# A two-block transformer on one core: wider loads of the experts' down weights, and a different last stretch

## The chip, the cores and the metric

The kernel runs on one core of one Trainium2 chip. The metric is the device time of one launch in microseconds (us), the median of several runs.

## The reference

The program is one layer of each of two transformer blocks on 256 tokens of width 1024, in float32. The change touches only the last part, a mixture of 16 experts (`ec_moe`) and the final normalization:

```python
x = x + ec_moe(rmsnorm_2(x, norm_ffn_g), router_w, expert_w_gu, expert_w_down)
return rmsnorm_2(x, final_norm_g)

def ec_moe(h, router_w, w_gu, w_down):        # h: 256 x 1024, 16 experts, cap = 32 tokens for each
    aff = softmax(h @ router_w)
    gates, idx = top_k(aff.T, cap)            # each expert picks its 32 tokens
    xs = h[idx]                               # 16 x 32 x 1024
    for each expert e:
        ga, up = split(xs[e] @ w_gu[e])       # w_gu[e]: 1024 x 4096, 16 MB
        y[e] = (silu(ga) * up) @ w_down[e]    # w_down[e]: 2048 x 1024, 8 MB
    return scatter-add of gates * y to the picked tokens
```

All 16 experts work, so 384 MB of expert weights are read once.

## The kernel before

`Body.run` goes through block 1, block 2's mixers and cross attention, and then `moe` (from L1209). In `moe` the 32 tokens of an expert are the stationary operand and the weights stream through TensorE, so that each weight is read once by a matmul of 512 columns. Four such matmuls sit side by side in the array (`tile_position=(0, 32 * j)`).

For each expert the code (L1271 to L1367) does the following.
- Every fourth expert gathers the tokens of four experts with one-hot matmuls (`gather`, L1284) into `xs`.
- Gate and up weights (`w_gu`): from the third expert on, four loads of 4 MB (L1303), each giving every partition 32 KB in one piece. Each load feeds 32 matmul instructions (L1314; a float32 matmul is two instructions in the trace).
- SiLU on ScalarE (L1334), the product on VectorE (L1335), four transposes of 128 x 128 (L1338) and a copy give `aT`, the activations with features on partitions. Feature `512 j + 4 p + c` of the expert lies on partition p, block c.
- Down weights (`w_down`): four loads of 2 MB (L1365), each giving every partition 16 KB. `down` (L1342) feeds each to 16 matmul instructions (L1347), which sum into two PSUM banks `y`.
- `scatter` (L1355): the two banks are copied to SBUF, one by ScalarE (L1357), one by VectorE (L1359), and a one-hot matmul with the gates (L1361) adds them into four PSUM banks `acc` that stay open over the experts.

`eload` (L1228) issues each load from SyncE, which here does nothing but issue DMAs, in program order. A load waits until the last reader of its buffer is done. Buffers come from `slots`: four of 32 KB per partition (`e_`) and four of 16 KB (`hl`, the pool `big` that block 1 and 2 used). One expert uses each once.

The order of the other instructions on each engine is made by a scheduler at build time. `queued` and `issue_after` put an instruction behind a named one, and `strict` keeps program order on PE, VectorE and ScalarE.

The last expert (e = 15) is different. After expert 14, `acc` is added to `x` on VectorE (L1374). The gain row of the last normalization is loaded and spread over partitions (L1377 to L1381). Then the down weights come as two loads of 2 MB (j = 0, 1), and j = 2 and 3 in column pieces: `cuts` are 512, 256, 128 and 128 columns (L1386, L1401). For each cut the result goes through `scatter`, is added to `x` (L1410), squared and summed (L1411). After the last cut VectorE works out the reciprocal root of both token blocks together by a bit trick and three Newton steps (`rstd`, L1415), ScalarE scales the left half and VectorE the right half (L1417, L1418), and two DMAs write the output (L1420).

Of the kernel before, what the change touches and what calls it, by code (L numbers as in the profile page):

```python
# [9 lines left out]
F32 = mybir.dt.float32  # L10
# [22 lines left out]
class Body:  # L33
# [223 lines left out]
    def rstd_q(self, ss):  # L257

        nc = self.nc
        q = self.small.tile([128, 8], F32, name="rstq", tag="rsq", bufs=4)  # L260
        v, d, h, y, t = (q[:, i:i + 1] for i in range(5))
        nc.vector.tensor_scalar(v, ss[:, 0:1], ss[:, 1:2], 1.0 / D, OP.add, OP.mult)
        nc.scalar.activation(d, v, AF.Sqrt, bias=self.eps)
        nc.vector.tensor_scalar(h, v, -0.5, -0.5 * EPS, OP.mult, OP.add)
        nc.vector.reciprocal(y, d)
        nc.vector.tensor_scalar(t, y, y, h, OP.mult, OP.mult)
        nc.vector.tensor_scalar(y, t, 1.5, y, OP.add, OP.mult)
        return y
# [29 lines left out]
    def run(self):  # L298
# [10 lines left out]
        self.big = self.open("big", 1)  # L309
# [896 lines left out]
    def moe(self):  # L1206
# [3 lines left out]
        with ExitStack() as es:  # L1210
            ep, x = self.ep, self.x
            ew = self.open("ew", 1, es)
# [58 lines left out]
            for e in range(NE):  # L1271
                q = e % 4
                if q == 0:
# [60 lines left out]
                nc.scalar.activation(s, G, AF.Silu, scale=rs)  # L1334
                nc.vector.scalar_tensor_tensor(s, U, rs, s, OP.mult, OP.mult)  # L1335
                p = self.ps()
                for c in range(4):
                    nc.tensor.transpose(p[:, c * 128:(c + 1) * 128], s[:, c:512:4], self.ident)  # L1338
                aT = ew.tile([128, 4, 128], F32, name="aT", tag="aT")
                nc.scalar.activation(aT.rearrange("p c s -> p (c s)"), p, AF.Copy)  # L1340
# [8 lines left out]

                def rows(j):  # L1350
                    return wdn[e, 512 * j:512 * j + 512].rearrange("(p i) n -> p i n", i=4)


                def scatter(c0, n, out, first, last):
                    ys = ew.tile([128, n], F32, name="ys", tag="ys")  # L1355
                    if c0 == 0:
# [3 lines left out]
                    for t in range(2):  # L1360
                        nc.tensor.matmul(out[t], ogT[:, t * 128:(t + 1) * 128], ys, start=first, stop=last)  # L1361

                if e < NE - 1:
                    for j in range(4):
                        raw = eload(rows(j).rearrange("p i n -> p (i n)"))  # L1365
                        for n in range(2):
                            down(j, raw, 512 * n, 512)  # L1367
                    for n in range(2):
                        scatter(512 * n, 512, acc[n::2], e == 0, e == NE - 2)

            for t in range(2):
                for n in range(2):
                    c = slice(512 * n, 512 * n + 512)
# [94 lines left out]
```

## Time and profile before

| | us |
|---|---|
| median of 3 runs (lowest to highest) | 1518.48 (1516.9 to 1519.0) |
| profiled execution, its own device time | 1518.31 |
| span of the profiled execution, first to last instruction | 1516.6 |
| PE busy | 1162.6 (77%) |
| VectorE busy | 424.4 (28%) |
| ScalarE busy | 355.5 (23%) |

The span leaves 1.7 us of the execution's time outside it. Blocks 1 and 2 take the first 560 us or so; the expert loop takes the remaining 950 us. A busy PE in the table is an average over both. The page's slices show that the two parts differ: PE is busy 90% or more of nearly all of the first part, and 50 to 60% of the second, where the DMA engines stand at 9 tenths or more in every slice but the last.

In the rows further down, times are us from the start of the span. A row of the timeline has start, duration, engine, source line, operation, the written and the read tiles, the shape and the number of instructions that were merged; in brackets stands how long the engine had been idle and what ended the wait.

### The profile page before, as it was taken

To read this page: it belongs to the slowest core of one execution; us is meant where nothing else is said; L and a number is where in the kernel's file an instruction comes from. 1 tells how busy PE (TensorE), PEld (TensorE's weight loads), DVE (VectorE), ACT (ScalarE), POOL (GpSimd) and SP (SyncE) were. 2 spreads that over 40 slices of the span, in tenths; PEclk is the share of its full clock that TensorE was granted. 3 is DMA by queue.
4 is the path that set the end of the run, shared out by engine and by line. 5 is a ranking of instruction groups with operands and counts; after the bars stand their busy time and mean duration, and the time that the engine had idled before them with its cause. 6 is when DMAs were issued, how large, how long until landed. Compare 5 with 4: busy or idle time off the path is not lost.

```text
span 1516.6 us, 17752 instructions
## 1 busy us (share of the span) xinstructions
PE 1162.6 (77%) x7704; PEld 690.8 (46%) x7704; DVE 424.4 (28%) x801; ACT 355.5 (23%) x614; POOL 7.0 (0%) x19
## 2 busy tenths in 40 slices
PE   7999999999999999885665656665656656556665
PEld 5989989999988776321121111121111112111112
DVE  6744567445568864200000000000000000000002
ACT  6545546434456733000000000000000000000002
POOL 1000000000000000000000000000000000000000
PEclk9999999999999999997888877889888889888788
DMA  9754538555643279999999999999999999999996
GB/s 304 226 167 139 167 116 273 182 184 191 201 131 99 85 293 423 393 430 428 433 431 425 432 425 434 429 427 433 429 428 431 430 427 434 430 426 432 427 431 239
DMA packets 98189, 502.98 MB, mean 332 GB/s; under 512 B 8107, under 2 KB 62143, under 8 KB 80960
## 3 DMA queue, kind: packets, MB, share of 16 engines
q1 hardware_dynamic: 98112, 501.85, 82.6%
q8 instruction: 60, 0.98, 0.3%
q14 instruction: 17, 0.14, 0.0%
HBM read 500.79 MB, written 1.05 MB: 331 GB/s over the span
## 4 chain that ended last, share of the span: by engine, by line
PE 70%; another core or an unknown queue 16%; DMA 5%; DVE 3%; SPq 2%; ACT 2%; issue 1%; DVEq 0%; ACTq 0%
PE acc L127 21%; PE sm L1314 18%; PE sm L127 10%; PE sm L1347 9%; PE acc L1361 4%; DMA eraw<-in_expert_w_down_dram 2%; DMA eraw<-in_expert_w_gu_dram 2%; SPq L1401 2%; PE sm L1284 1%; PE acc L1171 1%; PE sm L1338 1%; DVE es L1335 1%; DVE ys L1359 1%; ACT aT L1340 1%
## 5 line engine op out<-in xcount | busy, mean ns | idle before, releaser
L1314 PE MATMUL sm<-eraw,xs 128*32 128x512 f32 x2048 | 319.0, 779 | 222.9 <-DMA eraw<-in_expert_w_gu_dram 222.9
L1314 PEld LDWEIGHTS sm<-eraw,xs 128*32 128x32 f32 x2048 | 77.0, 138 | 447.4 <-issue 230.8
L74 DVE TENSOR_TENSOR whl<-raw,whl 128x1024 fp32r<-128x1024 f32 x152 | 181.7, 1221 | 105.9 <-ACT whl L73 104.8
L1347 PE MATMUL sm<-eraw,aT 128*32 128x512 f32 (+2 forms) x1088 | 145.1, 669 | 66.2 <-DMA eraw<-in_expert_w_down_dram 54.5
L73 ACT ACTIVATE whl<-raw 128x1024 fp32r<-128x1024 f32 x152 | 154.0, 1052 | 78.0 <-issue 47.2
L1335 DVE SCALAR_TENSOR_TENSOR es<-sm,rsl,es 128x512 f32<-128x512 f32 x16 | 12.0, 751 | 439.5 <-PE sm L1314 436.6
L1334 ACT ACTIVATE es<-sm,rsl 128x512 f32<-128x512 f32 x16 | 11.0, 687 | 408.4 <-PE sm L1314 408.4
L1347 PEld LDWEIGHTS sm<-eraw,aT 128*32 128x32 f32 x1088 | 32.5, 120 | 161.5 <-DMA eraw<-in_expert_w_down_dram 89.6
L127 PE MATMUL acc<-xh,whl 128*128 128x256 f32 x704 | 96.2, 285 | 0.0
L127 PE MATMUL sm<-xh,whl 128*128 128x256 f32 x704 | 91.4, 283 | 0.0
L127 PEld LDWEIGHTS acc<-xh,whl 128*128 128x128 f32 x704 | 88.4, 189 | 1.1
L127 PEld LDWEIGHTS sm<-xh,whl 128*128 128x128 f32 x704 | 87.9, 189 | 0.6
L1361 PE MATMUL acc<-ys,ogT 128*128 128x512 f32 (+2 forms) x136 | 65.2, 603 | 15.2 <-DVE ys L1359 14.4
L1359 DVE COPY ys<-sm 128x512 f32<-128x512 f32 (+2 forms) x18 | 11.4, 631 | 196.9 <-PE acc L1361 196.9
L127 PE MATMUL acc<-whl,xh 128*128 128x512 f32 x240 | 65.9, 405 | 0.2
L1332 ACT ACTIVATE ogT<-sm 128x256 f32<-128x256 f32 x16 | 6.1, 383 | 220.6 <-PE sm L1330 220.6
L127 PE MATMUL acc<-whl,aH 128*128 128x512 f32 x176 | 55.9, 390 | 0.0
L1357 ACT ACTIVATE ys<-sm 128x512 f32<-128x512 f32 x16 | 9.6, 597 | 196.5 <-PE sm L1347 196.5
L1361 PEld LDWEIGHTS acc<-ys,ogT 128*128 128x128 f32 x136 | 23.2, 193 | 59.8 <-DVE ys L1359 27.7
L127 PE MATMUL acc<-xl,whl 128*128 128x256 f32 x352 | 50.1, 283 | 0.0
L127 PEld LDWEIGHTS acc<-whl,xh 128*128 128x128 f32 x240 | 44.6, 190 | 10.9 <-ACT xh L162 0.8
L127 PE MATMUL sm<-xl,whl 128*128 128x256 f32 x352 | 49.4, 283 | 0.0
(392 smaller groups left out, 1171.6 us busy)
## 6 DMA issues: line engine op xcount, KB each, us to landing
eraw<-in_expert_w_gu_dram SPq DMA_DIRECT2D x56, 4096.0 KB, 53.0
eraw<-in_expert_w_down_dram SPq DMA_DIRECT2D x62, 2048.0 KB, 55.2
raw<-in_w_in_dram SPq DMA_DIRECT2D x34, 1024.0 KB, 5.4
eraw<-in_expert_w_gu_dram SPq DMA_DIRECT2D x16, 2048.0 KB, 16.1
raw<-in_w_gate_dram SPq DMA_DIRECT2D x11, 1024.0 KB, 5.3
raw<-in_w_up_dram SPq DMA_DIRECT2D x11, 1024.0 KB, 5.6
raw<-in_w_down_dram SPq DMA_DIRECT2D x11, 1024.0 KB, 5.0
raw<-in_w_out_dram SPq DMA_DIRECT2D x8, 1024.0 KB, 5.1
```

The source lines that it names most:

```text
L73: nc.scalar.activation(H[:, k], raw[:, k], AF.Copy)
L74: self.at["L"] = nc.vector.tensor_tensor(L[:, k], raw[:, k], H[:, k].bitcast(F32), OP.subtract).ins
L127: nc.tensor.matmul(out, l[i], r[j], start=first and p == 0 and q == 0, stop=last and p == 2 and q == n - 1)
L1171: nc.tensor.matmul(acc[c], o[:, k, t * 128:(t + 1) * 128], w[c][:, k, :], start=k == 0, stop=k == 3)
L1284: nc.tensor.matmul(pg[kk][:, i * 128:(i + 1) * 128], x[:, t, feats(k)], OH[:, t, e:e + 4, :].rearrange("p e s -> p (e s)"), start=t == 0, ...
L1314: nc.tensor.matmul(dst[32 * j:32 * j + 32, :], xs[:, k, 32 * q:32 * q + 32], raw[:, o + 512 * j:o + 512 * j + 512], start=k == 0, stop=k = ...
L1335: nc.vector.scalar_tensor_tensor(s, U, rs, s, OP.mult, OP.mult)
L1338: nc.tensor.transpose(p[:, c * 128:(c + 1) * 128], s[:, c:512:4], self.ident)
L1347: nc.tensor.matmul(y[c0][32 * c:32 * c + 32, 0:n], aT[:, c, 32 * j:32 * j + 32], raw[:, o:o + n], start=j == 0, stop=j == 3, tile_position ...
L1359: nc.vector.tensor_copy(ys, y[c0][:, 0:n])
L1361: nc.tensor.matmul(out[t], ogT[:, t * 128:(t + 1) * 128], ys, start=first, stop=last)
L1401: nc.sync.dma_start(raws[j].rearrange("p (i n) -> p i n", i=4)[:, :, c0:c0 + m], rows(j)[:, :, c0:c0 + m])
```

## The change

1. Experts 4 to 14 (`wide`) read their down weights in two loads of 4 MB, 32 KB for each partition, where four loads of 2 MB were. Before expert 4 the pools `ew` and `big` are closed, two buffers of 32 KB (`d0`, `d1`) take the place of the four of 16 KB, and `ew4` that of `ew`.
2. In such a load partition p holds the rows `1024 j + 8 p + i`. So `aT` needs 64 features of each 512-wide block per partition half: 16 matmuls of 64 columns with parts of the identity replace the four transposes. `down2` uses the same number of matmuls as `down` did.
3. The residual `x` is added into `acc` after expert 3 by four matmuls with the identity; `acc` stays open to expert 15. The additions on VectorE at L1374 and L1410 go.
4. The last expert loads j = 0 to 2 whole and j = 3 in two halves of 512 columns. For j = 3 and what follows the order is strict. Squares and the product with the gain are read from PSUM for all four halves; the last copy out of `y` is shared by VectorE and ScalarE. `rstd_q` (square root on ScalarE, reciprocal, one Newton step) takes the place of `rstd`, for both token blocks in turn. A square root of a constant is issued behind the last SiLU. VectorE's last step is a product with a per-partition scalar (`tensor_scalar`) instead of one with two operands.

```diff
-    def rstd_q(self, ss):
+    def rstd_q(self, *sums):
...
+        for ss in sums:
             v, d, h, y, t = (q[:, i:i + 1] for i in range(5))
             nc.vector.tensor_scalar(v, ss[:, 0:1], ss[:, 1:2], 1.0 / D, OP.add, OP.mult)
             nc.scalar.activation(d, v, AF.Sqrt, bias=self.eps)
             nc.vector.tensor_scalar(h, v, -0.5, -0.5 * EPS, OP.mult, OP.add)
+        for d, h, y, t in qs:
             nc.vector.reciprocal(y, d)
             nc.vector.tensor_scalar(t, y, y, h, OP.mult, OP.mult)
             nc.vector.tensor_scalar(y, t, 1.5, y, OP.add, OP.mult)
...
+                wide = 4 <= e < NE - 1
+                if e == 4:
+                    self.close(ewst, self.bigst)
+                    slots[4:] = [(self.open("d%d" % i, 1, self.bigst), "d", 1) for i in range(2)]
+                    n_unit[0] = 0
+                    ew = self.open("ew4", 1, ewst)
...
+                if wide:
+                    idn = self.ident.rearrange("p (a b c) -> p a b c", a=2, b=2)
+                    for i in range(8):
+                        for b in range(2):
+                            nc.tensor.matmul(p[64 * b:64 * b + 64, 64 * i:64 * i + 64], s[:, i:512:8], idn[:, :, b, :],
+                                             start=True, stop=True, tile_position=(0, 64 * b))
...
+                def down2(j, raw, c0):
+                    for i in range(8):
+                        c, o = i % 4, 1024 * i + c0
+                        nc.tensor.matmul(y[c0][32 * c:32 * c + 32, :], aT[:, i, j, :], raw[:, o:o + 512],
+                                         start=j == 0 and i < 4, stop=j == 1 and i >= 4, tile_position=(0, 32 * c))
...
+                    if e == NE - 1 and c0:
+                        nc.vector.tensor_copy(ys[:, 0:256], y[c0][:, 0:256])
+                        nc.scalar.activation(ys[:, 256:512], y[c0][:, 256:512], AF.Copy)
...
+                if wide:
+                    for j in range(2):
+                        raw = eload(wdn[e, 1024 * j:1024 * j + 1024].rearrange("(p i) n -> p (i n)", i=8), 8192)
+                        for n in range(2):
+                            down2(j, raw, 512 * n)
...
+                if e == 3:
+                    for t in range(2):
+                        for n in range(2):
+                            nc.tensor.matmul(acc[2 * t + n], self.ident, x[:, t, 512 * n:512 * n + 512],
+                                             start=False, stop=False)
...
+            with self.queued([silu]):
+                nc.scalar.activation(fo[:, 0, 0:1], self.eps, AF.Sqrt)
+            raws = [w[:, o:o + 4096] for w in (slot(8192), slot(8192)) for o in (0, 4096)]
+            for j in range(3):
+                nc.sync.dma_start(raws[j], rows(j).rearrange("p i n -> p (i n)"))
+                for n in range(2):
+                    down(j, raws[j], 512 * n, 512)
+            for n in range(2):
+                c = slice(512 * n, 512 * n + 512)
+                nc.sync.dma_start(raws[3].rearrange("p (i n) -> p i n", i=4)[:, :, c], rows(3)[:, :, c])
+            with self.strict():
+                for n in range(2):
+                    c = slice(512 * n, 512 * n + 512)
+                    down(3, raws[3], 512 * n, 512)
+                    scatter(512 * n, 512, acc[n::2], False)
+                    for t in range(2):
+                        nc.scalar.activation(junk, acc[2 * t + n], AF.Square, accum_out=ss[t][:, n:n + 1])
+                        nc.vector.tensor_tensor(fo[:, t, c], acc[2 * t + n], g[:, c], OP.mult)
+                r = self.rstd_q(*ss)
                 for t in range(2):
+                    nc.scalar.activation(fo[:, t, 0:512], fo[:, t, 0:512], AF.Copy, scale=r[t])
+                    nc.vector.tensor_scalar(fo[:, t, 512:D], fo[:, t, 512:D], r[t], None, OP.mult)
+                    nc.sync.dma_start(self.out[t * 128:(t + 1) * 128, :], fo[:, t, :])
```

## Rows read from the trace of the kernel before

**Rows 1.** Windows; columns: engines' busy us, then granted clock, DMA share, GB/s.

```profile
1300.00:1400.00 100.00, 59.74 (x388) 15.95 (x380) 4.05 (x8) 4.53 (x8) 0.00 (x0) 0.86 1.01 430
...
1497.00:1502.40 5.40, 4.32 (x48) 1.84 (x51) 1.98 (x3) 1.32 (x3) 0.00 (x0) 1.00 0.54 178
...
850.60:854.20 3.60, 3.60 (x16) 0.57 (x16) 0.00 (x0) 0.00 (x0) 0.00 (x0) 0.50 1.07 455
```

**Rows 2.** DMA issues: count, KB each, median us from issue to landing.

```profile
eraw<-in_expert_w_gu_dram SPq DMA_DIRECT2D x56, 4096.0 KB, 53.0
eraw<-in_expert_w_down_dram SPq DMA_DIRECT2D x62, 2048.0 KB, 55.2
```

**Rows 3.** Timeline of PE through one whole expert, first gate load to the next expert's.

```profile
688.48 5.02 PE L1314 MATMUL sm<-eraw,xs 128*32 128x512 f32 x32 [3.14 <-DMA eraw<-in_expert_w_gu_dram]
...
707.84 5.34 PE L1314 MATMUL sm<-eraw,xs 128*32 128x512 f32 x32 [4.40 <-DMA eraw<-in_expert_w_gu_dram]
717.56 5.84 PE L1314 MATMUL sm<-eraw,xs 128*32 128x512 f32 x32 [4.38 <-DMA eraw<-in_expert_w_gu_dram]
724.33 0.75 PE L1338 MATMUL sm<-ident,es 128*128 128x128 f32 x4 [0.94 <-DVE es L1335]
725.83 3.64 PE L1347 MATMUL sm<-eraw,aT 128*32 128x512 f32 x32 [0.75 <-ACT aT L1340]
732.25 3.60 PE L1347 MATMUL sm<-eraw,aT 128*32 128x512 f32 x16 [2.78 <-DMA eraw<-in_expert_w_down_dram]
737.15 1.92 PE L1347 MATMUL sm<-eraw,aT 128*32 128x512 f32 x16 [1.29 <-DMA eraw<-in_expert_w_down_dram]
...
746.95 3.64 PE L1314 MATMUL sm<-eraw,xs 128*32 128x512 f32 x16 [3.13 <-DMA eraw<-in_expert_w_gu_dram]
```

**Rows 4.** The same view in a later expert, around a late landing.

```profile
834.48 5.34 PE L1314 MATMUL sm<-eraw,xs 128*32 128x512 f32 x32 [4.57 <-DMA eraw<-in_expert_w_gu_dram]
...
850.58 3.64 PE L1347 MATMUL sm<-eraw,aT 128*32 128x512 f32 x16 [4.39 <-DMA eraw<-in_expert_w_down_dram]
```

**Rows 5.** Timeline of all engines from the last gate load to the last product.

```profile
1482.14 5.84 PE L1314 MATMUL sm<-eraw,xs 128*32 128x512 f32 x32 [4.38 <-DMA eraw<-in_expert_w_gu_dram]
...
1497.30 1.06 PE L1347 MATMUL sm<-eraw,aT 128*32 128x512 f32 x8 [1.28 <-DMA eraw<-in_expert_w_down_dram]
1498.49 0.60 ACT L1357 ACTIVATE ys<-sm 128x512 f32<-128x512 f32 x1 [6.28 <-PE sm L1347]
...
1499.14 1.98 PE L1361 MATMUL acc<-ys,ogT 128*128 128x512 f32 x4 [0.78 <-ACT ys L1357]
...
1501.06 1.73 PE L1347 MATMUL sm<-eraw,aT 128*32 128x256 f32 x40
...
1503.02 0.42 DVE L1359 COPY ys<-sm 128x256 f32<-128x256 f32 x1
...
1508.13 0.19 ACT L1411 ACTIVATION_READ_ACCUMULATOR eraw<-x 128x1 f32 x1
...
1510.71 1.42 DVE L1418 SCALAR_TENSOR_TENSOR eraw<-x,rstd,eraw 128x512 f32<-128x512 f32 x2
```

**Rows 6.** Timeline of ScalarE and VectorE at an earlier call of `rstd_q`.

```profile
417.07 0.60 ACT L254 ACTIVATE pj<-acc 128x512 bf16<-128x512 f32 x1 [4.84 <-PE acc L127]
...
418.51 1.28 ACT L263 ACT_TABLE_LOAD   x1
...
423.36 0.21 DVE L262 TENSOR_SCALAR rstq<-ss 128x1 f32<-128x1 f32 x1
...
423.60 0.29 ACT L263 ACTIVATE rstq<-rstq,eps 128x1 f32<-128x1 f32 x1 [0.38 <-DVE rstq L262]
...
424.44 0.21 DVE L267 TENSOR_SCALAR rstq<-rstq 128x1 f32<-128x1 f32 x1
```

**Rows 7.** VectorE's groups by form: products of an SBUF tile with per-partition scalars.

```profile
L1111 DVE TENSOR_SCALAR aE<-aE,st 128x256 f32<-128x256 f32 x24 | 7.6, 349 | 0.2
...
L420 DVE TENSOR_SCALAR vs<-vs,mv,rstd 128x1024 f32<-128x1024 f32 x2 | 1.6, 811 | 0.0
```

More of the change, by code (lines that the diff above doesn't have):

```diff
@@ L255, in squares @@
         return ss
-    def rstd_q(self, ss):
+    def rstd_q(self, *sums):
         nc = self.nc
[L260 to L268, printed above, removed]
+        qs = []
+        for ss in sums:
+            q = self.small.tile([128, 8], F32, name="rstq", tag="rsq", bufs=4)
+            v, d, h, y, t = (q[:, i:i + 1] for i in range(5))
+            nc.vector.tensor_scalar(v, ss[:, 0:1], ss[:, 1:2], 1.0 / D, OP.add, OP.mult)
+            nc.scalar.activation(d, v, AF.Sqrt, bias=self.eps)
+            nc.vector.tensor_scalar(h, v, -0.5, -0.5 * EPS, OP.mult, OP.add)
+            qs.append((d, h, y, t))
+        for d, h, y, t in qs:
+            nc.vector.reciprocal(y, d)
+            nc.vector.tensor_scalar(t, y, y, h, OP.mult, OP.mult)
+            nc.vector.tensor_scalar(y, t, 1.5, y, OP.add, OP.mult)
+        return y if len(sums) == 1 else [q[2] for q in qs]
     def xh(self, t):
@@ L1333, in moe @@
                 s = ew.tile([128, 512], F32, name="es", tag="es")
-                nc.scalar.activation(s, G, AF.Silu, scale=rs)
+                silu = nc.scalar.activation(s, G, AF.Silu, scale=rs).ins
                 nc.vector.scalar_tensor_tensor(s, U, rs, s, OP.mult, OP.mult)
                 p = self.ps()
[L1337 to L1340, printed above, removed]
+                if wide:
[4 more added lines that the diff above has]
+                                             start=True, stop=True, tile_position=(0, 64 * b))
+                else:
+                    for c in range(4):
+                        nc.tensor.transpose(p[:, c * 128:(c + 1) * 128], s[:, c:512:4], self.ident)
+                aT = ew.tile([128, 8, 2, 32], F32, name="aT", tag="aT")
+                nc.scalar.activation(aT.rearrange("p i j s -> p (i j s)"), p, AF.Copy)
+                if not wide:
+                    aT = aT.rearrange("p i j s -> p (i j s)").rearrange("p (c s) -> p c s", c=4)
                 y = {0: self.ps(), 512: self.ps()}
@@ L1360, in scatter @@
                     for t in range(2):
-                        nc.tensor.matmul(out[t], ogT[:, t * 128:(t + 1) * 128], ys, start=first, stop=last)
-                if e < NE - 1:
+                        nc.tensor.matmul(out[t], ogT[:, t * 128:(t + 1) * 128], ys, start=first, stop=e == NE - 1)
+                if wide:
[3 more added lines that the diff above has]
+                            down2(j, raw, 512 * n)
+                elif e < NE - 1:
                     for j in range(4):
@@ L1424, in consts @@
+            self.close(est, ewst, self.bigst)
 def consts():
```

57 lines of the change are left out of this document (10 added, 47 removed).

## The prediction

> **What bounds the kernel now.** I read the windows first, to see which resource is full in the expert loop. In a stretch of 100 us in its middle the DMA engines are busy all the time and move 430 GB/s, while PE works 59.7 us of 100, and VectorE and ScalarE under 5 each [rows 1]. The DMA issues come second: a load lands 53 to 55 us after its issue [rows 2], about one expert's time, so some 22 MB are always queued. The timeline of PE comes third: each matmul group of an expert waits for a landing, 3 to 4 us at a time, and catches up with it [rows 3]. So until the last byte has landed the time is bytes over rate, and work on an engine costs nothing while the queue stays full. Only two things can move the end: the rate at which the loads run, and the chain after the last landings.
>
> **Part 1, the loads.** A 4 MB load takes 9.72 us (717.56 less 707.84), one expert 58.47 us (746.95 less 688.48) [rows 3]. Six loads of 4 MB would take 6 x 9.72 = 58.32 us, so the four loads of 2 MB cost 0.15 us more than two of 4 MB would. The other reading of the same rows: 737.15 less 732.25 is 4.90 us for 2 MB, so a pair costs 9.80 and two pairs 0.16 us more [rows 3]. For 11 experts that is 1.6 to 1.8 us; the new load has the shape of the gate load (32 KB for each partition in one piece), so I take its time from there and book 1.6 us. Row times are rounded to 0.01 us and a PE start trails its landing by up to 0.1, which makes the low end 1.1 us.
>
> The Trainium skill has a rule for this in "DMA: Bandwidth & Descriptors", section "Anatomy of one DMA": a DMA takes some 2.0 us fixed plus its bytes at 436 GB/s, fitted for the GpSimd path. By it a 2 MB load would take an estimated 6.8 us and a 4 MB load 11.6, and the change would save 4 us for each expert, 44 us in all. The trace disagrees: 4.90 and 9.72 us, since the fixed part of a queued load lies under the load ahead of it.
>
> The change moves readers and waits, and none of them reaches the queue. A 4 MB buffer comes free when both halves are read. PE reads 2 MB in 1.92 us at full clock and 3.60 at half [rows 3], so the reuse of a buffer moves by one landing and one such read at most, 4.90 + 3.60 = 8.5 us, out of 53. On SyncE's queue the loads of the next expert stand behind it; they lose the same 8.5 us and still come some 44 us ahead. Closing the pools before expert 4 makes `d0` wait for two old buffers instead of one, the same 8.5 us. The four float32 transposes become 16 matmuls, 32 instructions where an ordinary matmul takes two. They are not in the trace; the bounds are 0.75 us (four transposes now) and 32 x 0.19 = 6.0 us, with the price of one 128-column transpose for each [rows 3]. Halfway, 3.4, is my value, as the columns are half as many. The first down matmul starts 8.3 us after the last gate landing now (725.83 less 717.56), so then at 10.9 (13.5 at the dear end), against 9.72 for the landing: PE falls 1 to 4 us behind and has 9.72 us of the next load to catch up. Cost 0; if the queue were empty it would be up to 3.8 us for each expert. The four matmuls with the identity after expert 3 are 8 instructions, about 4 us by the 1.98 us of four [rows 5], hidden by the same queue, and the four additions on VectorE that go were hidden too.
>
> More PE instructions also mean more instruction fetches over the same DMA engines. I can't price one from a row. One landing in this loop came 1.41 us late (834.48 to 850.58 is 16.10 us, where 717.56 to 732.25 is 14.69 [rows 3, 4]). I don't know what made it; one such delay more or less is my bound, plus or minus 1.4 us.
>
> **Part 2, the end.** I set the last gate load at 1482.14 [rows 5] and count both ways to VectorE's last product, which ends at 1512.13 before (1510.71 plus 1.42). What follows, two output DMAs, is unchanged.
>
> The half loads of 1 MB: the landing that PE sees at 1497.30 is two loads of 2 MB and two of 1 MB after 1482.14, so a half takes (15.16 - 9.80) / 2 = 2.68 us [rows 3, 5]. In the new kernel j = 0 to 2 take 14.70, the first half of j = 3 lands at 1499.52 and the second at 1502.20.
>
> From there, all on the path, with durations of [rows 5]:
> - down, first half: 1.06, to 1500.58. Gap 0.13 and copy 0.60, to 1501.31; 0.05 to the scatter.
> - scatter of the first half from 1501.36. The strict order puts it ahead of the second half's down, which can follow 1.92 later (1501.06 less 1499.14): 1503.28. The second half has landed 1.1 us before, so PE, not the DMA, sets this point.
> - down, second half: 1.06, to 1504.34. Gap 0.23 and the shared copy at 0.42, to 1504.99; 0.05.
> - scatter 1.98, to 1507.02. Gap 0.1, then square and accumulator read side by side with the product, 0.60 + 0.19, to 1507.91.
> - reciprocal root: one token block takes 423.36 to 424.65 = 1.29 us [rows 6]. The second block adds its own five VectorE steps, about 1.1: 1510.3. The table of the square root, 1.28 us [rows 6], is loaded behind the last SiLU, while PE waits for weights, so it costs 0 here; without that cover it would be 1.28.
> - the last product, twice. 0.35 us for 256 elements and 0.81 for 1024 [rows 7] give about 0.50 for 512: to 1511.3.
>
> That is 0.8 us ahead of 1512.13. The removed work (narrow cuts, additions to x, Newton steps) goes, but a PE queue in fixed order and a second reciprocal root take most of it back. The ends: 1.6 us if the reciprocal roots of both blocks overlap fully and the gaps vanish; 0.5 us lost if each step pays 0.15 us more (nine steps).
>
> **Sum.** 1518.31 - 1.6 - 0.8 = 1515.9 for the profiled execution; the median lies 0.17 above that execution, so 1516.1.
>
> **The rivals.**
> (a) The clock falls in the tail. In the rows before, PE has work in 4.32 of the 5.40 us and its granted clock is 1.00 (2.4 GHz) [rows 1]. The new tail has three short bursts with waits between. After 2 to 4 us with nothing to do the clock stood at half (1.2 GHz) when work came: 16 instructions took 3.60 and 3.64 us against 1.92 [rows 1, 3, 4]. At half, j = 2's 16 instructions run 1.0 us into the first half's landing, two downs cost 0.86 more each and two scatters 1.8 each (half clock doubles 1.98 less its tail): 6.3 us, so 1522.4. It decides if the clock is at half when the first half of j = 3 lands, and only in full if it stays there through both halves. For it: PE's pause of about 2 us ahead of j = 2. Against it: the pauses are shorter than those in rows 3.
> (b) The loads give nothing: the 0.15 us for each expert belong to something else between the experts, not to the size of a load. Then only the tail is left: 1518.48 - 0.8 = 1517.7. Against it, 4.90 twice is over 9.72 in one and the same queue.
> (c) A load has a larger fixed cost than rows 3 show for full ones: the halves of 1 MB take 2.68 us where half of 4.90 is 2.45, 0.23 more each. With 0.23 for each of the 22 loads that go, 5.1 us, and 0.8: 1512.6. This is the page's rule as far as a row bears it out, though 2 KB pieces explain the 0.23 as well; at the page's own figure it would be some 1474, which I give under 1%.
> (d) It doesn't do what it says: the new pools make expert 4's loads wait for everything ahead, the queue runs dry once. It would need a wait of over 44 us, and each us beyond is lost; 5 us of it gives 1521.
>
> **How the numbers follow.** The forecast, 1516.1 with its own spread of 1.3 us (tail 1.6 to -0.5, one late landing), 0.77. (a) 0.07, (b) 0.06, (c) 0.07, (d) 0.03. A measurement of this kernel can tell about 0.2% (3.0 us) from no change, so faster means under 1515.4: 0.27 of the 0.77 by its spread, and (c), 0.34 together. Slower means over 1521.5: part of (a), (d) and a rest, 0.07. Within: 0.59. The range leaves out 0.1 on each side: it reaches down most of the way to (c), with the late landing taken away, and up past (b), with one late landing more: 1513.6 to 1518.8.
>
> **What would show it.** Two down landings of an expert should be 9.72 us apart, and a whole expert 58.3 us. The issue-to-landing time should stay above 40 us; if it falls below 10, (d) or the buffers are at work. The transposes of experts 4 to 14 should take 2 to 6 us, with PE late for the first down landing and early again for the next gate load. In the tail, the second half's down should wait for the scatter of the first and not for a DMA, and the granted clock should be 1.00; 0.50 there is (a). No table load should stand behind the last landing. The prediction is wrong if an expert takes less than 58.1 us or the tail moves by more than 2 us.

## The result, and the profile after

| | us |
|---|---|
| before, median of 4 runs taken beside the changed kernel (lowest to highest) | 1518.73 (1516.9 to 1519.0) |
| after, median of 4 runs (lowest to highest) | 1508.78 (1507.54 to 1509.52) |
| ratio, with its 95% interval | 0.9936 (0.9919 to 0.9953) |
| profiled execution, after | 1507.54, span 1505.83 |

The kernel became 9.95 us faster. That lies 7.3 us below the forecast and outside the range: the prediction was wrong. To find the place I cut the span of both profiled executions at three marks that exist in both: the first gate load of the third expert (the row at 688.48 in [rows 3]), the last gate load (1482.14 in [rows 5]), and the end of VectorE's last product.

| us | before | after | difference |
|---|---|---|---|
| start to the third expert's first gate load | 688.48 | 679.01 | -9.47 |
| from there to the last gate load | 793.66 | 792.31 | -1.35 |
| from there to the end of the last product | 29.99 | 29.74 | -0.25 |
| from there to the end of the span | 4.45 | 4.77 | +0.32 |
| span | 1516.58 | 1505.83 | -10.75 |

The two parts that the prediction priced gave 1.35 us and next to nothing. The rest was gained before the first changed instruction of the expert loop runs, most of it in blocks 1 and 2, whose instructions the diff leaves as they are (`rstd_q` with one argument issues the same six). The mark after, in PE's timeline:

```profile
679.01 3.64 PE L1327 MATMUL sm<-eraw,xs 128*32 128x512 f32 x32 [3.15 <-DMA eraw<-in_expert_w_gu_dram]
```

Blocks 1 and 2 are bound by PE. Most of their matmuls come from one line, L127 in both kernels. In the larger part of these, 128 x 128 weights (`whl`) are stationary and the 256 tokens (`xh`, or `xl` for the low part) move. The view of that line gives count, shortest, median and longest in ns, and the time of the first and the last. Before:

```profile
L127 PE MATMUL acc<-xh,whl x704: 274/282/384, 38.4 to 468.1; 128*128 128x256 f32 x176
L127 PE MATMUL sm<-xh,whl x704: 274/284/285, 239.1 to 408.3; 128*128 128x256 f32 x176
```

After:

```profile
L127 PE MATMUL acc<-xh,whl x704: 276/276/384, 38.3 to 459.9; 128*128 128x256 f32 x176
L127 PE MATMUL sm<-xh,whl x704: 276/281/384, 234.2 to 400.4; 128*128 128x256 f32 x176
```

The count is the same, the first starts at the same time, and the last one into `acc` comes 8.2 us earlier. The same work is done by shorter instructions: 6 ns less for those into `acc`, 3 ns for those into `sm`. Matmuls overlap, so what counts is the distance from start to start. PE's timeline shows it for groups of 16 + 8. Before:

```profile
67.58 2.06 PE L127 MATMUL acc<-xh,whl 128*128 128x256 f32 x16
69.48 1.11 PE L127 MATMUL acc<-xl,whl 128*128 128x256 f32 x8
70.43 2.06 PE L127 MATMUL acc<-xh,whl 128*128 128x256 f32 x16
```

After:

```profile
69.14 1.98 PE L127 MATMUL acc<-xh,whl 128*128 128x256 f32 x16
70.95 1.07 PE L127 MATMUL acc<-xl,whl 128*128 128x256 f32 x8
71.86 1.98 PE L127 MATMUL acc<-xh,whl 128*128 128x256 f32 x16
```

24 matmuls take 2.85 us before and 2.72 us after, 118.8 and 113.3 ns each. No wait stands between them in either kernel. There are 704 + 704 of them with `xh` and half as many with `xl`, 2112 in all. At 6 ns for the half that goes to `acc` and 2 to 3 for the half that goes to `sm` that would be 8.4 to 9.5 us, an estimate from the medians. The trace has 8.4: the last matmul of L127 of all starts at 575.4 us before and at 567.0 after. The other 1.1 us of the 9.47 lie between there and the mark, in the first two experts and what leads up to them. That stretch takes 113.1 us before and 112.0 after, and 111.7 to 114.7 over the kernels further down; why it varies was not tried.

The expert loop after. DMA issues (issuing engine, count, KB each, median us to landing), to be set beside [rows 2]:

```profile
eraw<-in_expert_w_gu_dram SPq DMA_DIRECT2D x56, 4096.0 KB, 53.2
eraw<-in_expert_w_down_dram SPq DMA_DIRECT2D x22, 4096.0 KB, 53.0
```

PE's timeline of a changed expert, to be set beside [rows 3]:

```profile
1119.80 6.04 PE L1327 MATMUL sm<-eraw,xs 128*32 128x512 f32 x32 [4.39 <-DMA eraw<-in_expert_w_gu_dram]
1126.78 2.14 PE L1355 MATMUL sm<-ident,es 128*64 128x64 f32 x32 [0.94 <-DVE es L1348]
1129.68 3.64 PE L1377 MATMUL sm<-eraw,aT 128*32 128x512 f32 x32 [0.76 <-ACT aT L1361]
1139.24 6.55 PE L1377 MATMUL sm<-eraw,aT 128*32 128x512 f32 x32 [5.92 <-DMA eraw<-in_expert_w_down_dram]
1145.73 1.98 PE L1394 MATMUL acc<-ys,ogT 128*128 128x512 f32 x4
1148.57 1.98 PE L1394 MATMUL acc<-ys,ogT 128*128 128x512 f32 x4 [0.85 <-DVE ys L1392]
1150.48 3.64 PE L1327 MATMUL sm<-eraw,xs 128*32 128x512 f32 x32
1158.67 1.85 PE L1327 MATMUL sm<-eraw,xs 128*32 128x512 f32 x8 [3.67 <-DMA eraw<-in_expert_w_gu_dram]
```

The queue is as full as before. The 32 instructions of the short transposes take 2.14 us; PE then waits for the copy of `aT` and not for the load, so it is a little late, waits for the next landing again (5.92 us), and is late once more for the next expert (1150.48, no wait) until 1158.67. From 1139.24 to 1158.67 are two landings, 19.43 us, 9.72 each. The next expert's load in the place of that at 1119.80 comes at 1178.11, so a whole expert takes 58.31 us, where the prediction has 58.3.

The end after, all engines but the weight loads, to be set beside [rows 5]:

```profile
1488.77 1.06 PE L1370 MATMUL sm<-eraw,aT 128*32 128x512 f32 x8 [0.75 <-DMA eraw<-in_expert_w_down_dram]
...
1490.61 1.98 PE L1394 MATMUL acc<-ys,ogT 128*128 128x512 f32 x4 [0.78 <-ACT ys L1390]
...
1492.52 1.07 PE L1370 MATMUL sm<-eraw,aT 128*32 128x512 f32 x8
...
1493.41 0.69 DVE L1442 TENSOR_TENSOR eraw<-acc,eraw 128x512 f32<-128x512 f32 x1 [0.23 <-ACT eraw L1441]
1494.02 0.41 DVE L1387 COPY ys<-sm 128x256 f32<-128x256 f32 x1
1494.47 0.38 ACT L1388 ACTIVATE ys<-sm 128x256 f32<-128x256 f32 x1 [1.09 <-DVE ys L1387]
1494.90 1.98 PE L1394 MATMUL acc<-ys,ogT 128*128 128x512 f32 x4 [1.31 <-ACT ys L1388]
...
1497.48 0.19 ACT L1441 ACTIVATION_READ_ACCUMULATOR eraw<-acc 128x1 f32 x1
1497.70 0.69 DVE L1442 TENSOR_TENSOR eraw<-acc,eraw 128x512 f32<-128x512 f32 x1 [0.23 <-ACT eraw L1441]
1498.31 0.20 DVE L264 TENSOR_SCALAR rstq<-ss 128x1 f32<-128x1 f32 x1
...
1500.19 0.87 DVE L1446 TENSOR_SCALAR eraw<-eraw,rstq 128x512 f32<-128x512 f32 x2
```

Two steps that were meant to run side by side run in turn here: the two halves of the shared copy (VectorE at 1494.02, ScalarE only at 1494.47), and each product behind its square (the wait for ScalarE at 1493.41 and 1497.70). In each pair both engines read one PSUM bank. In the kernel before, where square and product read `x` in SBUF, they start 0.06 us apart:

```profile
1501.02 0.63 ACT L1411 ACTIVATE eraw<-x 128x512 f32<-128x512 f32 x1 [1.94 <-DVE x L1410]
...
1501.08 0.69 DVE L1413 TENSOR_TENSOR eraw<-x,eraw 128x512 f32<-128x512 f32 x1
```

### The profile page after: what moved, and what is told of

Its sections match the earlier page's. It is cut to its first block, busy times and chain, and to the rows that moved or that the text cites. A ratio compares the mean times of both kernels' runs of the same rounds, so it can differ in the third digit from the quotient of the medians.

```text
span 1505.8 us, 18173 instructions
## 1 busy us (share of the span) xinstructions
PE 1176.1 (78%) x7948; PEld 699.6 (46%) x7948; DVE 418.1 (28%) x786; ACT 356.7 (24%) x611; POOL 7.0 (0%) x19
## 4 chain that ended last, share of the span: by engine, by line
PE 34%; another core or an unknown queue 15%; DMA 8%; DVE 2%; issue 1%; ACT 1%; SPq 0%; DVEq 0%; ACTq 0%
PE sm L1327 18%; DMA eraw<-in_expert_w_down_dram 8%; PE sm L1377 7%; PE acc L1394 4%; PE sm L1370 2%; PE sm L1355 2%; PE sm L1297 1%; DVE es L1348 1%; DVE ys L1392 1%; PE sm L1343 0%; ACT aT L1361 0%; PE acc L1413 0%; PE sm L1335 0%; DVE rsl L1338 0%
## 5 line engine op out<-in xcount | busy, mean ns | idle before, releaser
L1377 PE MATMUL sm<-eraw,aT 128*32 128x512 f32 x704 | 106.5, 760 | 63.5 <-DMA eraw<-in_expert_w_down_dram 59.4
L127 PE MATMUL acc<-xh,whl 128*128 128x256 f32 x704 | 93.2, 280 | 0.0
L127 PE MATMUL sm<-xh,whl 128*128 128x256 f32 x704 | 89.7, 280 | 0.0
L1377 PEld LDWEIGHTS sm<-eraw,aT 128*32 128x32 f32 x704 | 26.1, 135 | 133.4 <-issue 62.8
L127 PEld LDWEIGHTS sm<-xh,whl 128*128 128x128 f32 x704 | 86.1, 189 | 0.7
L127 PEld LDWEIGHTS acc<-xh,whl 128*128 128x128 f32 x704 | 85.5, 188 | 1.1
L1392 DVE COPY ys<-sm 128x512 f32<-128x512 f32 x15 | 10.4, 691 | 236.5 <-PE acc L1394 236.5
L1394 PE MATMUL acc<-ys,ogT 128*128 128x512 f32 x128 | 64.3, 625 | 14.0 <-DVE ys L1392 11.9
L127 PE MATMUL acc<-whl,xh 128*128 128x512 f32 x240 | 65.4, 403 | 0.2
L1370 PE MATMUL sm<-eraw,aT 128*32 128x512 f32 x320 | 45.8, 710 | 13.8 <-DMA eraw<-in_expert_w_down_dram 10.7
L127 PE MATMUL acc<-whl,aH 128*128 128x512 f32 x176 | 55.7, 389 | 0.0
L127 PEld LDWEIGHTS acc<-whl,xh 128*128 128x128 f32 x240 | 44.4, 190 | 10.4 <-ACT xh L162 0.8
L127 PE MATMUL acc<-xl,whl 128*128 128x256 f32 x352 | 48.5, 278 | 0.0
```

The lines of the kernel that those rows point to most:

```text
L127: nc.tensor.matmul(out, l[i], r[j], start=first and p == 0 and q == 0, stop=last and p == 2 and q == n - 1)
L1370: nc.tensor.matmul(y[c0][32 * c:32 * c + 32, 0:n], aT[:, c, 32 * j:32 * j + 32], raw[:, o:o + n], start=j == 0, stop=j == 3, tile_position ...
L1377: nc.tensor.matmul(y[c0][32 * c:32 * c + 32, :], aT[:, i, j, :], raw[:, o:o + 512], start=j == 0 and i < 4, stop=j == 1 and i >= 4, tile_p ...
L1392: nc.vector.tensor_copy(ys, y[c0][:, 0:n])
```

## The experiments

**Where the gain before the loop comes from.** One thing in the diff reaches blocks 1 and 2: the placement of tiles in SBUF. The old end called `rstd` for two token blocks at once. Its tile has a tag of its own ("rs2", two buffers of 32 bytes) in the pool `small`, which lives through the whole program and lies ahead of nearly everything. The new end calls `rstd_q`, whose tag block 2 uses already. So `small` is 64 bytes shorter, and each tile placed behind it lies 64 bytes lower on every partition: `whl` at byte 21280 where it was at 21344. `xh` is placed from the other end and stays at 212960. The distance between them, modulo 256 (the remainder when it is divided by 256), was 128 bytes and is 192. My theory was that this distance sets the spacing of the matmuls; the rivals were something else in the changed program, or the position of one tile alone. Five runs test that and do one part of the change at a time.

The changed kernel with 64 bytes of padding, which puts all tiles behind it back where they were:

```diff
         self.ep = self.open("ep", 1)
+        self.ep.tile([128, 16], F32, name="pad", tag="pad")
```

> The changed kernel, with 64 B for each partition put back as an unused tile ahead of the pool `ep`, so that the split weights (tile whl) lie at partition byte 21344 again, as in the kernel before, and not at 21280. Address theory: the 9.5 us that the trace of the changed kernel is ahead of the old one before the third expert come from these addresses alone; they go, the 256-column matmuls of L127 are back at 119 to 120 ns from start to start (113 to 118 in the changed kernel), and the time is 1516.5 to 1517.5 us. Rival (chip, or the longer instruction stream): the pad does nothing, 1508.8 us.

Measured: 1516.45 us, ratio to before 0.9987 (0.9978 to 0.9997). The third expert's first gate load starts at 687.42, and line L127 is as slow as before:

```profile
L127 PE MATMUL acc<-xh,whl x704: 274/282/384, 38.3 to 468.2; 128*128 128x256 f32 x176
```

The kernel before without the 64 bytes, and nothing else changed:

```diff
-        q = self.small.tile([128, 4, n], F32, name="rstd", tag=tag + str(n), bufs=4 if n == 1 else 2)
+        q = self.small.tile([128, 4, n], F32, name="rstd", tag=tag if n == 2 else tag + str(n), bufs=4 if n < 3 else 2)
...
-            r = self.rstd(ss[:, 10:12], 2, 1.0 / D)
+            r = self.rstd(ss[:, 10:12], 2, 1.0 / D, "st1")
```

> The kernel before, with its last reciprocal root in a buffer of the tag st1, so that the pool small is 64 B smaller and whl lies at 21280, as in the changed kernel; the same instructions in the same order. Address theory: about 9.5 us faster, 1509 us, with 113 to 118 ns from start to start of the 256-column matmuls of L127. Rival: no change, 1518.5 us, with 119 to 120 ns.

Measured: 1511.46 us, ratio 0.9955 (0.9940 to 0.9970); first gate load at 679.20.

```profile
L127 PE MATMUL acc<-xh,whl x704: 276/276/384, 38.2 to 460.2; 128*128 128x256 f32 x176
```

So 64 bytes in a pool carry the gain, with none of the intended change, and without them the intended change has little. The time is 2.5 us above the 1509 that were expected. The start of the loop is as expected; in the trace (of an execution of 1510.70 us) 0.5 us are lost between the third expert and the last gate load (794.19) and 1.15 behind it (31.14), at a granted clock of 0.79 from there to the end.

The same edit with `xh` and what lies behind it moved down by 64 bytes too:

```diff
+        self.xt.tile([128, 16], F32, name="xpad", tag="xpad", bufs=1)
```

> As the run before, and the right-hand tiles from the stationary or moving activations (xh, xl) on down by 64 B too, so that the distance from whl to xh is that of the kernel before while whl is at 21280. If the distance between the two operands sets the spacing: back to 119 to 120 ns and about 1518.5 us. If the address of whl in itself does: 113 to 118 ns, about 1509 us. If neither address matters: 1518.5 us with no difference to the run before.

Measured: 1518.93 us, first gate load at 688.53.

```profile
L127 PE MATMUL acc<-xh,whl x704: 274/281/387, 38.5 to 467.9; 128*128 128x256 f32 x176
```

`whl` lies at the same byte as in the fast kernels, and the time is that of before. So it is not the place of `whl` alone; the medians are those of before, whose distance it has. This is the only run in which `xh` moves.

**The two parts alone, at the old distance.** The loads alone (the pools, `wide`, `aT`, `down2` put into the kernel before), and the end alone (the changed kernel with `wide = False`, no pools closed, and the padding):

> The kernel before with part 1 alone: 4 MB down loads and 64-feature transposes for experts 4 to 14, the old end, and every tile of blocks 1 and 2 at its old address. Theory (the load part is worth its DMA time): the first gate loads of experts 3 and 15 lie 1.4 to 1.6 us closer together than before, and the time is 1517.1 us (1516.0 to 1518.0). Rival (large fixed cost of a load): 1513.7 us or less. Rival (the loads give nothing): 1518.7 us.

> The changed kernel with part 1 undone (2 MB loads, four transposes) and 64 B put back, so that every tile of blocks 1 and 2 is at its old address: the new end alone. Theory: from the last gate load to the last product 29.7 us, 0.25 less than before, as in the trace of the changed kernel; 1518.4 us (1517.3 to 1519.2). Rival (the end is what made the 2 us between the run with the pad and the kernel before): 1516.5 us.

| us | time | ratio | third expert to last gate load | last gate load to last product |
|---|---|---|---|---|
| before | | | 793.66 | 29.99 |
| loads alone | 1517.48 | 0.9989 (0.9980 to 0.9999) | 792.09 | 32.47 |
| end alone | 1517.61 | 0.9991 (0.9981 to 1.0001) | 793.66 | 29.58 |
| all, old distance (padding) | 1516.45 | 0.9987 (0.9978 to 0.9997) | 792.07 | 30.62 |
| all, as changed | 1508.78 | 0.9936 (0.9919 to 0.9953) | 792.31 | 29.74 |

In the traces the loads give 1.4 to 1.6 us in each of these three kernels, and nothing where they are not in. Over all 17 traces of this document that stretch takes 793.66 to 794.23 us in the five kernels with loads of 2 MB and 792.03 to 792.81 in the twelve with loads of 4 MB. By the medians the two parts alone give 1.3 and 1.1 us, and both together 2.3. The last column varies mostly for another reason: PE's clock. The windows from the last gate load to the end of the span (length, busy PE, PEld, VectorE, ScalarE, GpSimd, granted clock, DMA share, GB/s), for the changed kernel and for the one with padding:

```profile
1471.30:1505.83 34.53, 20.24 (x112) 5.55 (x112) 6.30 (x18) 9.63 (x20) 0.00 (x0) 0.85 0.55 222
```

```profile
1479.50:1514.90 35.40, 23.40 (x112) 6.28 (x112) 6.30 (x18) 9.63 (x20) 0.00 (x0) 0.74 0.53 218
```

Both run the same 112 matmul instructions; with padding PE needs 3.2 us more for them at the lower clock, falls behind the loads of j = 0 to 2, and the end is 0.9 us longer. The run with the loads alone has 0.73 in that stretch and an end 2.5 us longer. Before, the end alone and the changed kernel have 0.85. Each kernel has one trace, so the runs don't show whether that clock goes with the kernel or with the execution. Behind the first down of j = 3 the end doesn't vary: from there to the last product the changed kernel takes 12.29 us (1488.77 to 1501.06) and the end alone 12.29.

**Which distances are fast.** Eight more kernels set the distance in other ways: padding of 192, 32 or 96 bytes; 64 bytes added to the kernel before; and small tiles of the changed kernel that share or lose buffers. The edits, one line each:

```diff
# e4: before; e8, e11, e14: after, with 48, 8 and 24 elements
+        self.ep.tile([128, 16], F32, name="pad", tag="pad")
# e7
-                rs = self.small.tile([128, 1], F32, name="rsl", tag="st9", bufs=2)
+                rs = self.small.tile([128, 1], F32, name="rsl", tag="st1", bufs=4)
# e9; e10 has bufs=1 and the edit of e7 too
-            st = self.small.tile([128, 16], F32, name="rs", tag="st8", bufs=4)
+            st = self.small.tile([128, 16], F32, name="rs", tag="st8", bufs=2)
# e13
-                rs = self.small.tile([128, 1], F32, name="rsl", tag="st9", bufs=2)
+                rs = self.small.tile([128, 1], F32, name="rsl", tag="st9", bufs=1)
```

> The kernel before with 64 B more ahead of ep: whl at 21408, whose remainder by 128 is that of 21280. Address theory with a period of 128 B: about 1509 us, 113 to 118 ns. With a longer period: another time, from 1509 to 1530 us. If addresses don't matter: 1518.5 us and 119 to 120 ns.

> The changed kernel with 64 B less ahead of whl (the buffers of rsl taken from another tag): whl at 21216, its distance to xh 256 modulo 512 where it was 192 in the changed kernel and 128 in the kernel before. The same instructions in the same order. Theory: the distance sets the spacing, with no known order, so anything from 1500 to 1520 us; a time within 1 us of 1508.8 with 113 and 118 ns would say that only distances near 128 are bad.

> The changed kernel with 192 B more ahead of whl: distance from whl to xh a multiple of 512 (0). Where both operands moved together in the old kernel (whl against aH, distance 0 modulo 512) the 512-column matmuls were at 227 ns, against 231 to 235 at other distances. Theory: distance 0 is a good place, L127's matmuls at 118 ns or less, 1500 to 1510 us; if only a distance of 192 is good: 1514 to 1520 us.

> The changed kernel with 128 B less ahead of whl (two buffers fewer of the tag st8): distance from whl to xh 320 modulo 512. Theory (a distance that is an odd multiple of 64 B is fast, an even one slow, as 64 and 192 were against 0, 128 and 256): 113 to 118 ns from start to start of L127's 256-column matmuls and 1508 to 1514 us. Rival (only some distances near 192 are fast): 119 to 120 ns and 1516.5 us.

> The changed kernel with 256 B less ahead of whl: distance 448 modulo 512. Theory (odd multiples of 64 B are fast): 113 to 118 ns and 1508 to 1514 us. Rival: 119 to 120 ns and 1516.5 us.

> The changed kernel with 32 B more ahead of whl: distance 160 modulo 512, between the fast 192 and the slow 128. Theory (what counts is whether both operands share a place modulo 128 B): a value between, 115 to 119 ns and 1510 to 1515 us. Rival (anything but an odd multiple of 64 B is slow): 119 to 120 ns and 1516.5 us. Rival (only even multiples of 64 B are slow): 113 to 118 ns and 1509 us.

> The changed kernel with one 32-byte buffer less in the pool of small tiles: the distance from the stationary tile whl to the moving tile xh is 224 bytes modulo 512 instead of 192. Theory (period of 256 bytes, only distances that are an odd multiple of 64 are fast): 119 to 120 ns between the 256-column matmuls, the experts' third first gate load at about 687.5 us, 1516.3 us. Rival (speed changes smoothly between 192, fast, and 256, slow): 115 to 117 ns, 682 to 685 us, 1511 to 1514. Rival (the address doesn't matter, something else in the pool did): 1508.8 as the changed kernel.

> The changed kernel with 96 bytes of padding ahead of the stationary tiles: distance 96 bytes modulo 256, between 64 (117 to 118 ns, 1514.6 and 1515.9) and 128 (119 to 120 ns, 1516.4). Theory (only odd multiples of 64): 119 to 120 ns, about 1516.4 us. Rival (smooth): 118 to 119 ns, 1515 to 1516, which this run alone could hardly tell apart; the row of the matmul spacing then decides.

Measured, ordered by distance; the two medians are those of line L127 with `xh` moving, into `acc` and into `sm`. The time is a median for e1, e2 and the changed kernel, and one execution for the others:

| distance modulo 512 (modulo 256) | kernel | ns into acc, into sm | third expert's first gate load | time, us |
|---|---|---|---|---|
| 0 (0) | e8 | 283, 283 | 687.69 | 1516.56 |
| 256 (0) | e7 | 283, 283 | 687.22 | 1516.19 |
| 64 (64) | e4, end and loads of before | 279, 279 | 686.16 | 1515.90 |
| 320 (64) | e9 | 279, 279 | 685.49 | 1514.64 |
| 96 (96) | e14 | 281, 281 | 689.97 | 1518.21 |
| 128 (128) | e1 | 282, 284 | 687.42 | 1516.45 |
| 128 (128) | e3, kernel before with both tiles moved | 281, 284 | 688.53 | 1518.93 |
| 160 (160) | e11 | 281, 281 | 687.67 | 1516.19 |
| 192 (192) | changed kernel | 276, 281 | 679.01 | 1508.78 |
| 192 (192) | e2, end and loads of before | 276, 281 | 679.20 | 1511.46 |
| 448 (192) | e10 | 276, 281 | 679.05 | 1507.79 |
| 224 (224) | e13 | 281, 280 | 686.51 | 1514.42 |

Distances that are equal modulo 256 give equal medians in all three pairs (0 and 256, 64 and 320, 192 and 448). At 192 the first gate load comes some 8 us earlier than at the slow distances, at 64 about 2 us and at 224 about 1. The start of the last matmul of L127 shows the order better, since the stretch behind it varies by itself: 566.5 to 567.2 us at 192, 571.4 and 571.5 at 64, 573.6 at 224, 574.5 at 160, 575.2 to 575.6 at 128, 575.4 and 576.0 at 0, and 576.7 at 96. A single group of 24 doesn't show it: at 64 it takes 2.72 us (70.31 to 73.03 in e9), as at 192.

A period of 128 bytes (e4) and 0 as a good distance (e8) were misses. Odd multiples of 64 as fast distances held for e10 and missed e9's time by 0.6 us, and 160 (e11), where a value between was expected, came out like 128 (1516.19 us against 1516.45). The rule for the last two runs, only odd multiples of 64, came close for the spacing at 224 (24 matmuls in 2.84 us, 118.3 ns, against 119 to 120 expected) but not for its time, 1.9 us below what was expected; half of that is in the loop's start at 686.51. And 96 has the latest end of L127, though its medians lie between those of 64 and 128. So 192 modulo 256 is the fast distance of those tried at 32 bytes; a rule behind the others was not found.

**Why the end gave so little.** Two kernels reorder the last expert's end, both with the changed kernel's distances. In the first both half loads of j = 3 are multiplied before the first scatter, and VectorE copies the whole second half into a buffer of its own:

```diff
                 for n in range(2):
-                    c = slice(512 * n, 512 * n + 512)
                     down(3, raws[3], 512 * n, 512)
+                for n in range(2):
+                    c = slice(512 * n, 512 * n + 512)
                     scatter(512 * n, 512, acc[n::2], False)
...
-                    if e == NE - 1 and c0:
-                        nc.vector.tensor_copy(ys[:, 0:256], y[c0][:, 0:256])
-                        nc.scalar.activation(ys[:, 256:512], y[c0][:, 256:512], AF.Copy)
```

> The changed kernel with another order at its end: both down groups of j = 3 ahead of both scatters, and the second copy whole on VectorE into a buffer of its own, where two engines shared one PSUM bank. Theory (the end is set by PE's fixed order and by engines that take turns on one bank): from the last gate load to the last product 28.7 us (28.4 to 29.0) where the changed kernel has 29.74, and 1507.8 us. Rival (the last landing sets the end): 29.7 us and 1508.8.

Measured: 1509.24 us, ratio 0.9940 (0.9924 to 0.9957), and 31.32 us from the last gate load to the last product, 1.6 longer than in the changed kernel. A miss, and the timeline shows why:

```profile
1491.45 1.06 PE L1370 MATMUL sm<-eraw,aT 128*32 128x512 f32 x8 [1.60 <-DMA eraw<-in_expert_w_down_dram]
1492.45 1.98 PE L1391 MATMUL acc<-ys,ogT 128*128 128x512 f32 x4
...
1495.25 0.69 DVE L1440 TENSOR_TENSOR eraw<-acc,eraw 128x512 f32<-128x512 f32 x1 [0.23 <-ACT eraw L1439]
1495.86 0.68 DVE L1389 COPY eraw<-sm 128x512 f32<-128x512 f32 x1
1496.60 1.98 PE L1391 MATMUL acc<-eraw,ogT 128*128 128x512 f32 x4 [2.16 <-DVE eraw L1389]
```

The second down now runs ahead of the first scatter, as meant. But VectorE keeps program order, and there the copy stands behind the two products of the left half, so the second scatter waits 2.16 us for it. The second kernel moves both copies ahead of both scatters:

```diff
+                for n in range(2):
+                    evict(512 * n, 512, ys[n])
+                for n in range(2):
+                    c = slice(512 * n, 512 * n + 512)
+                    spread(ys[n], acc[n::2], False)
```

> The changed kernel with its addresses for whl and xh, and the last expert's end reordered: both half loads of j = 3 are multiplied first, then both copies out of PSUM are made, and the two scatters follow back to back. Theory (the end lost its gain to the order, the second down behind the first scatter and the copy behind the products): from the last gate load to the end of the last product 28.7 us (28.4 to 29.1) against 29.74, so about 1507.8 us. Rival (the engines taking turns on a PSUM bank set the end, whatever the order): 29.7 us or more, 1508.8 us or more.

The copy of the second half is whole on VectorE here too. Measured: 28.98 us from the last gate load to the last product, 0.76 less than in the changed kernel, and 1507.93 us, ratio 0.9935 (0.9918 to 0.9952). By the time alone it can't be told from the changed kernel; the trace shows the gain:

```profile
1488.19 1.07 PE L1370 MATMUL sm<-eraw,aT 128*32 128x512 f32 x8 [0.74 <-DMA eraw<-in_expert_w_down_dram]
...
1491.85 1.98 PE L1392 MATMUL acc<-ys,ogT 128*128 128x512 f32 x4
1491.99 0.69 DVE L1388 COPY eraw<-sm 128x512 f32<-128x512 f32 x1 [14.36 <-PE sm L1370]
...
1493.67 1.88 PE L1392 MATMUL acc<-eraw,ogT 128*128 128x512 f32 x4
...
1496.14 0.19 ACT L1448 ACTIVATION_READ_ACCUMULATOR eraw<-acc 128x1 f32 x1
1496.37 0.69 DVE L1449 TENSOR_TENSOR eraw<-acc,eraw 128x512 f32<-128x512 f32 x1 [0.17 <-ACT eraw L1448]
1496.98 0.20 DVE L264 TENSOR_SCALAR rstq<-ss 128x1 f32<-128x1 f32 x1
...
1498.85 0.87 DVE L1453 TENSOR_SCALAR eraw<-eraw,rstq 128x512 f32<-128x512 f32 x2
```

The scatters follow back to back (1491.85, 1493.67). The last square is summed at 1496.33, but the reciprocal root starts at 1496.98, behind the last product on VectorE, which had itself waited for that square. From the first down of j = 3 to the last product it is 11.53 us (1488.19 to 1499.72), against 12.29. So the new order, with the copy in one piece, is worth 0.76 us, and taking turns still costs 0.65 at this place.

## Why the prediction was wrong, point by point

**The step that failed** is one that has no sentence of its own: that only two things can move the end, the rate of the loads and the chain after the last landings. That holds from the third expert on. It leaves out when the loop begins, and so takes blocks 1 and 2 as unchanged because no line of theirs is in the diff. They are bound by PE, so any change in the spacing of their matmuls moves the whole loop. That PE is full in that part could be seen (the section on the profile before says so), and the diff shows that a call to `rstd` goes. What can't be read from either is that a 64-byte buffer is worth 7.7 us (1516.45 less 1508.78). The prediction's ends and rivals all lie behind 688 us, so none of them could hold the result. Rival (c) came nearest in its time, at 1512.6, and is wrong in its mechanism: the loads alone gave 1.6 us, not 5.1.

**The loads** were right. Forecast 1.6 us (1.1 the low end); measured 1.35 in the changed kernel, 1.57 alone, 1.59 with padding. The late landing that was allowed for as chance plays no part: both traces have three of them. The prediction set a rule of the Trainium skill against the trace, from "DMA: Bandwidth & Descriptors", section "Anatomy of one DMA": by the fixed 2.0 us for each DMA that it gives the estimate was 44 us. A full queue on SyncE shows 1.6.

**Transposes, waits, queue** were right. Transposes 2.14 us (forecast 0.75 to 6.0, value 3.4), PE late for one landing and early again for a later one, though by 0.2 us where 1 to 4 were forecast (1129.68 less 1119.80 is 9.88, against 9.72), and 53.0 us from issue to landing. So rival (d), a queue that runs dry, and rival (b), loads that give nothing, fall.

**The end** was forecast at 29.16 us from the last gate load to the last product and measured at 29.74. By its terms: to the first scatter 19.22 forecast, 19.29 measured. From the end of the second down to the second scatter 0.70 forecast, 1.31 measured (1493.59 to 1494.90): the copy starts behind a product on VectorE, and its two halves take 0.41 and 0.38 us in turn. From that scatter to the reciprocal root 2.87 forecast, 3.41 measured, since the products wait for the squares. Reciprocal root and last product 3.4 forecast, 2.75 measured (1498.31 to 1501.06): the two blocks overlap better than forecast. And the output, which the prediction took as unchanged, took 0.32 us longer. That goes with the new end (4.62 to 4.78 us in every kernel that has it, 4.31 to 4.46 in those with the old one); its cause is open. The Trainium skill has the rule that the prediction missed, in "PSUM — Partial Sum Buffer", section "PSUM bank collisions raise a hardware error": two engines may not touch one bank at the same time in the same partitions, not even to read it, and the compiler's scheduler puts one behind the other. The rows at 1494.02 and 1494.47 agree: 0.83 us where 0.42 was booked. No run puts the two reads into different banks, so that the bank is the reason rests on these rows, on those of the kernel before, and on that rule.

**The clock, rival (a)**, was right as a mechanism and at the wrong place. In the changed kernel the stretch of scatters and downs for which it was feared runs at full clock (granted clock 1.00), and a scatter takes 1.98 us there:

```profile
1490.00:1498.00 8.00, 4.96 (x16) 1.51 (x16) 2.70 (x5) 3.69 (x10) 0.00 (x0) 1.00 0.04 14
```

Where the clock did fall the price was near: in the kernel before without the 64 bytes the first scatter took 3.42 us, 1.4 more than 1.98, where the prediction has 1.8.

```profile
1490.43 3.42 PE L1361 MATMUL acc<-ys,ogT 128*128 128x512 f32 x4 [0.78 <-ACT ys L1357]
```

In the new end the difference lies ahead of that stretch, at the loads of j = 0 to 2. There the clock differs between the traces (0.85 and 0.74 over the end). The first scatter then starts 20.18 us behind the last gate load with padding, where the changed kernel has 19.29; with the loads alone, and the old end, the end is 2.5 us longer than before.

With the old distance the whole change gives 1516.45 us, beside a forecast of 1516.1. That closeness is partly luck: the loads are as forecast, the stretch from the last gate load to the end of the span is 1.0 us longer than before instead of 0.8 shorter, and its third expert starts 1.1 us earlier (687.42 against 688.48), within what kernels at the same distance differ by (687.42 to 689.81). The part that wasn't priced (7.7 us) was three times as large as the whole gain that was forecast (2.4).

## What to carry to other kernels

Look at where a change moves tiles, not only at which instructions it touches: in a part that is bound by PE, compare the median of the unchanged matmuls before you explain a gain by what was edited. Put the tiles of before back with a few bytes of padding as the first experiment, since it separates placement from the change in one run. And where two engines read one PSUM bank, book them one behind the other.

## What the runs showed of the hardware

- The spacing of the matmuls of L127 with 256 moving columns (f32 in the trace, float32r in the kernel) depends on the distance in bytes between the stationary and the moving tile, modulo 256: 113.3 ns in one stretch at 192, 118.8 at 128, with no wait in the trace. That it is the distance and not the place of `whl` alone rests on the one run in which both moved. Over blocks 1 and 2 that is some 8.4 us. The Trainium skill, "SBUF — State Buffer", section "Who interferes with whom", gives TensorE one read port for the moving operand and an independent one for the weights, and puts all contention on the ports that VectorE and GpSimd share. It names no cost of placement. The kernel with 64 bytes less shows one: ratio 0.9955. Which part of the chip makes the difference no run here shows.
- The best distance depends on the role. With `whl` moving (512 columns) and `xh` stationary the median durations are 389 ns at a distance of 0, 392 to 394 at 192, 393 at 128 and 397 at 96. Here 0 is best, which is slow for the others.
- Some landings come late by 1.4 to 1.5 us, three between the third expert and the last gate load in either kernel, and at about even distances: before at 850.58, 1110.29 and 1374.92, after at 836.42, 1071.27 and 1296.33. In the changed kernel the load behind this gate load took 11.26 us instead of 9.72 (825.16 to 836.42), with the next down load on time behind it:

```profile
825.16 6.58 PE L1327 MATMUL sm<-eraw,xs 128*32 128x512 f32 x32 [3.39 <-DMA eraw<-in_expert_w_gu_dram]
832.68 2.20 PE L1355 MATMUL sm<-ident,es 128*64 128x64 f32 x32 [0.94 <-DVE es L1348]
836.42 6.07 PE L1377 MATMUL sm<-eraw,aT 128*32 128x512 f32 x32 [1.54 <-DMA eraw<-in_expert_w_down_dram]
846.05 6.38 PE L1377 MATMUL sm<-eraw,aT 128*32 128x512 f32 x32 [3.56 <-DMA eraw<-in_expert_w_down_dram]
```

  What makes them late wasn't tried. The table of the square root was loaded behind the last SiLU (1.28 us from 1477.31) and off the path, as forecast.
